# Two product-key expert layers: 64 down units during routing, both token tiles routed at once, one-hot rows token by token

## The chip, the cores and the metric

The kernel runs on one core of a Trainium2 chip, as one program of some 65,000 instructions. The metric is the device time of one execution in microseconds (us), the median of a few runs. The engines are named as the profile names them: PE is the Tensor engine (PEld its weight loads), DVE the Vector engine, ACT the Scalar engine, POOL GpSimd, SP the queue that issues the loads.

## The reference

256 tokens of width 1024 pass through two blocks. The first block has two layers, each a mixer and then a product-key expert layer, `peer_ffn`; the second block has no experts and is not touched here. The expert layer, cut to what matters:

```python
q = (xi @ w_query).reshape(B, PEER_CHUNK, PEER_HEADS, 2, PEER_HALF)     # 8 heads, 2 halves
s = jnp.einsum('bthpd,hpnd->bthpn', q, sub_keys)                         # 128 keys per half
s1, i1 = lax.top_k(s[..., 0, :], PEER_TOPK)                              # 16 best of each half
s2, i2 = lax.top_k(s[..., 1, :], PEER_TOPK)
cand = (s1[..., :, None] + s2[..., None, :]).reshape(..., 256)
top_s, top_c = lax.top_k(cand, PEER_TOPK)                                # 16 best pairs
idx = i1[top_c // 16] * 128 + i2[top_c % 16]
g = jax.nn.softmax(top_s, axis=-1)
act = jax.nn.gelu(einsum('btd,bthkd->bthk', xi, expert_down[idx]))
out = einsum('bthk,bthkd->btd', g * act, expert_up[idx])
```

There are 128 x 128 experts, and each of the 256 tokens chooses 8 x 16 of them.

## The kernel before

All experts are computed for all tokens, and the choice enters as a gate. The down and the up matrix are streamed in 128 units of 128 experts each, 512 KB a unit. One unit makes 24 matmuls of 256 columns: 8 chunks of the contraction, times three, since weights and data are split exactly into two parts, `whi`/`wlo` and `xnh`/`xnl` (`mm3`, L167 to L172). `Stream.unit` (L87) loads a unit (`raw`), ACT makes `whi` from it (L93), and DVE or POOL makes `wlo` = raw - whi (L97); the letters of `pattern` ("g" POOL, "v" DVE) say which of the two, unit by unit. `raw`, `whi` and `wlo` have three buffers each.

`peer` (L488) has four stretches.

1. *Query and scores.* 16 units of `wq` are multiplied with the tokens into `mm` banks. For every unit and each of two token tiles of 128, DVE looks for the 16 best of 128 scores: `top16`, five big instructions (L521 to L525) with three small loads of values.
2. *Ranks and keys.* For one token tile after the other: 54 candidate sums `cand`, `top16` over them for each of 8 heads, softmax gates `gt`, and the place in the candidate list turned into a pair of ranks `ra`, `rb` (L577 to L584), then into key numbers `key` by comparing with `iota`, multiplying and summing over `oh` (L593 to L599). PE transposes the result (`tp`) and DVE copies it to `it`: key numbers and gates with the tokens along the free axis.
3. *Down units kept.* The first `N_STORE` down units are multiplied during the first two stretches. Two units share a PSUM bank `dn`, ACT applies gelu and leaves them in `ca` (L607).
4. *One-hot.* For each of 64 groups of 4 tokens: `oa` is the one-hot row of the first key, `ob` that of the second key times the gate; PE multiplies the two (`gps`, L639, four products of 128 columns, each recorded as two matmuls), which gives the gate of every expert for each token. DVE multiplies the part of the kept units into `ca` (L641), ACT copies the rest to `gg` (L642). In every third group (`by_act`) ACT makes `ob` itself. `oa` and `ob` have three buffers.

L641 reads and writes a group's columns of all kept units at once, so no group can get past L641 before the last kept unit's gelu, and four banks for `gps` bound how far PE gets ahead. PE fills this stretch with `mod` matmuls of the second block (32 steps of four in layer 0) and with four "parked" down units (`N_PARK`). After it, down units that are left alternate with up units (`acc`), then up units alone, each 24 matmuls.

A scheduler sets the order of the instructions on each engine, by the order in which they are written, their dependencies and its own idea of how long they take; on the chip each engine works through its list in that order.

Of the kernel before, what the change touches and what calls it, by code (L numbers as in the profile page):

```python
# [22 lines left out]
N_STORE = 32  # L23
# [21 lines left out]
PAT_R = "g"  # L45
# [20 lines left out]
class Stream:  # L66
    """Weights streamed in tiles of 1024 columns, each split exactly in two float32r parts."""
# [33 lines left out]
class Net:  # L101
# [50 lines left out]
    def psum(self, **bufs):  # L152
        """the 8 banks by tag: "ac" accumulators, "fl" work for idle engines, the others in turn"""
# [25 lines left out]
    def proj_tok(self, ap, xn, out):  # L179
        """out[:, tt, :] = tokens x 256 columns, from two units of 4 contraction chunks."""  # L180
# [38 lines left out]
    def norm_stat(self, x, nr):  # L219
        """reciprocal root mean squares of the rows, on every partition"""  # L220
# [30 lines left out]
    def columns(self, r, pool):  # L251
        """rows of r (all alike) as one column per token tile"""
# [7 lines left out]
    def norm(self, x, gain, shift=None, pool=None, nr=None, r=None):  # L260
        """RMS-normalised rows, transposed, in two parts."""
# [42 lines left out]
# ------------------------------------------------------------------ first block, layer 0 mixer  # L304
def hgrn_gmlp(n: Net):
# [3 lines left out]
    with ExitStack() as st:  # L309
# [11 lines left out]
        # lower bound: first row of a softmax over three rows  # L321
# [38 lines left out]
        # scores S[s, h, t] by doubling blocks: every exponent is a sum of logs of f, never positive  # L360
# [51 lines left out]
        # token-major values of both halves  # L412
# [74 lines left out]
# ------------------------------------------------------------------ product-key experts  # L487
def peer(n: Net, layer, mod, mod_upto):  # L488
# [4 lines left out]
    with ExitStack() as st:  # L493
# [13 lines left out]
        with ExitStack() as sr:  # L507
# [6 lines left out]
            val = [r.tile([128, 16, 16], F32, name=f"val{t}") for t in range(2)]  # L514
            idx = [r.tile([128, 16, 16], U32, name=f"idx{t}") for t in range(2)]
            idf = [r.tile([128, 16, 16], F32, name=f"idf{t}") for t in range(2)]
            topv = [r.tile([128, 8, 16], F32, name=f"topv{t}") for t in range(2)]
            topc = [r.tile([128, 8, 16], U32, name=f"topc{t}") for t in range(2)]
# [8 lines left out]
            def score(j, qt):  # L527
# [4 lines left out]
                for tt in range(2):  # L532
                    tmp = r2.tile([128, 128], F32, tag="tmp", name="tmp")
                    top16(val[tt][:, j], idx[tt][:, j], sc[:, tt], tmp)
# [11 lines left out]
            score(*late)  # L546
            for tt in range(2):
                cand = r.tile([128, 8, NCAND], F32, tag="cand", name="cand")
                v4 = val[tt].rearrange("p (h s) k -> p h s k", s=2)
                for a0, a1, wb, o in CAND:  # L550
                    na = a1 - a0
                    nc.vector.tensor_tensor(
                        out=cand[:, :, o:o + na * wb].rearrange("p h (a b) -> p h a b", b=wb),
                        in0=v4[:, :, 0, a0:a1].unsqueeze(3).to_broadcast([128, 8, na, wb]),
                        in1=v4[:, :, 1, 0:wb].unsqueeze(2).to_broadcast([128, 8, na, wb]), op=OP.add)
                for h in range(8):
                    tmp = r2.tile([128, 128], F32, tag="tmp", name="tmp")
                    top16(topv[tt][:, h], topc[tt][:, h], cand[:, h], tmp[:, 0:NCAND])
                # gates
                gt = r.tile([128, 8, 16], F32, tag="gt", name="gt")  # L560
                gs = r.tile([128, 8], F32, tag="gs", name="gs")
                nc.vector.tensor_tensor(out=gt, in0=topv[tt], in1=topv[tt][:, :, 0:1].to_broadcast([128, 8, 16]),
                                        op=OP.subtract)
                nc.scalar.activation(out=gt, in_=gt, func=AF.Exp, scale=rc[:, tt:tt + 1])
                nc.vector.tensor_reduce(out=gs, in_=gt, axis=AX.X, op=OP.add)
                nc.vector.reciprocal(out=gs, in_=gs)
                nc.vector.tensor_tensor(out=gt, in0=gt, in1=gs.unsqueeze(2).to_broadcast([128, 8, 16]), op=OP.mult)
                # positions in the candidate list -> rank pairs -> key indices
                pos = r.tile([128, 8, 16], F32, tag="pos", name="pos")
                ra = r.tile([128, 8, 16], F32, tag="ra", name="ra")  # L570
# [1068 lines left out]
```

## Time and profile before

| | |
|---|---|
| median of 3 runs | 3510.65 us (3499.51 to 3512.86) |
| span of the profiled execution | 3511.2 us |
| PE busy | 3303.3 us, 94% of the span |
| DVE busy | 2213.6 us, 63% |
| ACT busy | 1665.6 us, 47% |
| POOL busy | 527.8 us, 15% |
| share of PE in the chain that ended last | 80%, of DVE 13% |

The span of the profiled execution stands for its whole time; nothing of note lies around it, and it is within 0.02% of the median. A busy PE is not one at its peak: matmuls are pipelined, and a record lasts about 0.28 us where the next one starts 0.117 us later. So matmuls are counted here, not added up. [...]

### The profile page before, as it was taken

How to read it: one execution, taken by the hardware profiler on the slowest of the kernel's cores; microseconds unless marked ns; L12 is line 12 of the kernel's file. 1: busy time of each engine (PE TensorE's matmuls, PEld its weight loads, DVE VectorE, ACT ScalarE, POOL GpSimd, SP SyncE). 2: the span in 40 equal slices, each digit the busy share in tenths (PEclk: the TensorE clock that was granted, in tenths of full speed). 3: DMA queues.
4: the chain of work that ended last, by engine and by line, in shares of the span. 5: the costliest groups of instructions: out<-in, count | busy, mean ns of one | idle time of the engine just before them, and what ended most of it. 6: DMA issues, size and time to landing. Idle time of an engine off the chain costs nothing.

```text
span 3511.2 us, 65248 instructions
## 1 busy us (share of the span) xinstructions
PE 3303.3 (94%) x26734; PEld 3151.3 (90%) x26734; DVE 2213.6 (63%) x4081; ACT 1665.6 (47%) x2613; POOL 527.8 (15%) x275
## 2 busy tenths in 40 slices
PE   7897989999999989699999999999999989999798
PEld 6787879999999779678999999899999779999698
DVE  6379785555555649887555555666675756666665
ACT  5444564444444344365444444544654544454443
POOL 2256430000000227541000000200000010100200
PEclk9998999999999999899999999999999989999899
DMA  6643545555555544365555555554444235455353
GB/s 223 231 155 117 169 160 185 199 186 181 185 182 187 199 156 150 104 201 195 200 184 182 185 182 185 198 186 159 144 163 156 91 108 187 161 184 167 130 183 108
DMA packets 165755, 597.75 MB, mean 170 GB/s; under 512 B 18512, under 2 KB 20176, under 8 KB 165072
## 3 DMA queue, kind: packets, MB, share of 16 engines
q1 hardware_dynamic: 165456, 593.59, 50.4%
q8 instruction: 209, 3.42, 0.4%
q14 instruction: 90, 0.74, 0.1%
HBM read 592.47 MB, written 1.05 MB: 169 GB/s over the span
## 4 chain that ended last, share of the span: by engine, by line
PE 80%; DVE 13%; ACT 2%; DMA 2%; issue 1%; POOL 1%; SPq 0%; ACTq 0%; DVEq 0%; POOLq 0%
PE acc L170 10%; PE acc L171 10%; PE acc L172 10%; PE ff L170 6%; PE ff L171 6%; PE ff L172 6%; PE dn L171 6%; PE dn L172 6%; PE dn L170 6%; PE mm L170 2%; PE mm L171 2%; PE mm L172 2%; DVE oa L621 2%; PE gps L639 2%; PE mod L940 1%
## 5 line engine op out<-in xcount | busy, mean ns | idle before, releaser
L93 ACT CAST whi<-raw 128x1024 fp32r<-128x1024 f32 x973 | 1015.6, 1046 | 1457.5 <-PE acc L171 541.7
L97 DVE TENSOR_TENSOR wlo<-raw,whi 128x1024 fp32r<-128x1024 f32 x812 | 999.7, 1232 | 839.7 <-ACT whi L93 839.4
L97 POOL TENSOR_TENSOR wlo<-raw,whi 128x1024 fp32r<-128x1024 f32 x161 | 392.7, 2446 | 2151.1 <-ACT whi L93 2131.5
L172 PE MATMUL dn<-xnh,wlo 128*128 128x256 f32 x2048 | 586.7, 287 | 11.4 <-POOL wlo L97 11.4
L170 PE MATMUL dn<-xnh,whi 128*128 128x256 f32 x2048 | 586.7, 286 | 4.0 <-ACT whi L93 4.0
L171 PE MATMUL dn<-xnl,whi 128*128 128x256 f32 x2048 | 585.6, 286 | 0.0
L171 PE MATMUL acc<-cl,whi 128*128 128x256 f32 x2048 | 570.4, 283 | 0.8 <-DVE cl L165 0.8
L172 PE MATMUL acc<-ch,wlo 128*128 128x256 f32 x2048 | 569.5, 283 | 0.0
L170 PE MATMUL acc<-ch,whi 128*128 128x256 f32 x2048 | 543.5, 283 | 0.0
L170 PE MATMUL ff<-xnh,whi 128*128 128x258 f32 x1760 | 505.2, 288 | 8.3 <-ACT whi L93 2.3
L171 PE MATMUL ff<-xnl,whi 128*128 128x258 f32 x1760 | 503.5, 286 | 7.7 <-DVE xnl L247 7.7
L172 PE MATMUL ff<-xnh,wlo 128*128 128x258 f32 x1760 | 500.6, 285 | 3.2 <-POOL wlo L97 1.9
L172 PEld LDWEIGHTS dn<-xnh,wlo 128*128 128x128 f32 x2048 | 398.9, 195 | 12.4 <-POOL wlo L97 12.4
L170 PEld LDWEIGHTS dn<-xnh,whi 128*128 128x128 f32 x2048 | 398.8, 195 | 4.8 <-ACT whi L93 4.8
L171 PEld LDWEIGHTS dn<-xnl,whi 128*128 128x128 f32 x2048 | 398.7, 195 | 0.0
L171 PEld LDWEIGHTS acc<-cl,whi 128*128 128x128 f32 x2048 | 393.4, 192 | 1.3 <-DVE cl L165 1.3
L172 PEld LDWEIGHTS acc<-ch,wlo 128*128 128x128 f32 x2048 | 393.1, 192 | 0.0
L170 PEld LDWEIGHTS acc<-ch,whi 128*128 128x128 f32 x2048 | 377.4, 192 | 0.0
L170 PEld LDWEIGHTS ff<-xnh,whi 128*128 128x128 f32 x1760 | 335.7, 191 | 12.9 <-ACT rstd L216 3.6
L171 PEld LDWEIGHTS ff<-xnl,whi 128*128 128x128 f32 x1760 | 338.1, 192 | 9.6 <-DVE xnl L247 9.0
L172 PEld LDWEIGHTS ff<-xnh,wlo 128*128 128x128 f32 x1760 | 336.4, 191 | 4.3 <-POOL wlo L97 2.1
L171 PE MATMUL acc<-hl,whi 128*128 128x256 f32 x880 | 245.8, 281 | 3.1 <-DVE hl L1017 3.1
(446 smaller groups left out, 5578.2 us busy)
## 6 DMA issues: line engine op xcount, KB each, us to landing
raw<-l_down SPq DMA_DIRECT2D x256, 512.0 KB, 3.3
raw<-l_up SPq DMA_DIRECT2D x256, 512.0 KB, 3.3
mraw<-w_mod SPq DMA_DIRECT2D x144, 512.0 KB, 4.3
raw<-f1i SPq DMA_DIRECT2D x132, 512.0 KB, 3.4
raw<-f2i SPq DMA_DIRECT2D x88, 512.0 KB, 4.1
raw<-f1o SPq DMA_DIRECT2D x66, 512.0 KB, 3.5
raw<-w_t SPq DMA_DIRECT2D x46, 512.0 KB, 4.0
raw<-f2o SPq DMA_DIRECT2D x44, 512.0 KB, 3.8
```

Source lines behind the costliest of these rows:

```text
L93: nc.scalar.copy(hi[:, 0:k], raw[:, 0:k])
L97: eng.tensor_tensor(out=low[:, 0:k], in0=raw[:, 0:k], in1=hi.bitcast(F32)[:, 0:k], op=OP.subtract)
L170: mm(out, w[0], x[0], start=first, stop=False, skip_group_check=True)
L171: mm(out, w[0], x[1], start=False, stop=False, skip_group_check=True)
L172: mm(out, w[1], x[0], start=False, stop=last, skip_group_check=True)
L621: nc.vector.tensor_tensor(out=dst, in0=n.iota.unsqueeze(1).to_broadcast([128, 4, 128]), in1=it[:, s, t0:t0 + 4].unsqueeze(2).to_broadcast( ...
L639: nc.tensor.matmul(g[:, t], a[:, t], b[:, t], start=t == 0, stop=True, skip_group_check=True)
L940: nc.tensor.matmul(ps[32 * j:32 * j + 32], n.cond[:, k], raw[:, j * T:(j + 1) * T], start=k == 0, stop=k == NDC - 1, tile_position=(0, 32 ...
```

## The change

`N_STORE` goes from 32 to 64: 64 down units are kept in `ca` and `gg` holds 64 in place of 96. `PAT_R` goes from "g" to "v": while an expert layer routes, DVE makes `wlo`, not POOL. The second stretch works on both token tiles at once: tiles of 16 rows (2 tiles x 8 heads) take the place of two rounds of 8, the ranks come from 18 instructions of 256 columns (before: 44 of 128 columns in each round), and `it` is complete only at the end. In the fourth stretch each token gets an instruction of its own for `oa` and for `ob`, with the key (and the gate) as one number per partition; the product with the gate by POOL is gone. Docstrings and comments are removed as well, which is left out here.

```diff
-N_STORE = 32
+N_STORE = 64
...
-PAT_R = "g"
+PAT_R = "v"
...
-            for tt in range(2):
-                cand = r.tile([128, 8, NCAND], F32, tag="cand", name="cand")
...
-                for a in range(2, 16):
-                    step = r2.tile([128, 8, 16], F32, tag="step", name="step")
-                    nc.vector.tensor_scalar(out=step, in0=pos, scalar1=float(starts[a][0]), scalar2=None, op0=OP.is_ge)
-                    nc.vector.tensor_tensor(out=ra, in0=ra, in1=step, op=OP.add)
-                    nc.vector.scalar_tensor_tensor(out=rb, in0=step, scalar=-float(starts[a - 1][1]), in1=rb,
-                                                   op0=OP.mult, op1=OP.add)
...
+            cand = r.tile([128, 16, NCAND], F32, name="cand")
...
+            nc.vector.tensor_scalar(out=ra, in0=pos, scalar1=-float(starts[8]), scalar2=0.0, op0=OP.add, op1=OP.max)
+            nc.vector.scalar_tensor_tensor(out=rb, in0=ra, scalar=-1.0, in1=pos, op0=OP.mult, op1=OP.add)
+            for a0, a1, wb, o in CAND[:-1]:
+                run = r.tile([128, 16, 16], F32, tag="run", name="run", bufs=2)
+                for i, s0 in enumerate(starts[a0 + 1:a1 + 1]):
+                    if i == 0:
+                        nc.vector.tensor_scalar(out=run, in0=pos, scalar1=float(s0), scalar2=None, op0=OP.is_ge)
+                    else:
+                        nc.vector.scalar_tensor_tensor(out=run, in0=pos, scalar=float(s0), in1=run,
+                                                       op0=OP.is_ge, op1=OP.add)
+                nc.vector.tensor_tensor(out=ra, in0=ra, in1=run, op=OP.add)
+                nc.vector.scalar_tensor_tensor(out=rb, in0=run, scalar=-float(wb), in1=rb, op0=OP.mult, op1=OP.add)
...
-                def equal(s, dst):
-                    nc.vector.tensor_tensor(out=dst, in0=n.iota.unsqueeze(1).to_broadcast([128, 4, 128]),
-                                            in1=it[:, s, t0:t0 + 4].unsqueeze(2).to_broadcast([128, 4, 128]),
-                                            op=OP.is_equal)
...
-                    equal(1, b)
-                    nc.gpsimd.tensor_tensor(out=b, in0=b, op=OP.mult,
-                                            in1=it[:, 2, t0:t0 + 4].unsqueeze(2).to_broadcast([128, 4, 128]))
+                for t in range(4):
+                    at = lambda s: it[:, s, t0 + t:t0 + t + 1]
+                    nc.vector.tensor_scalar(out=a[:, t], in0=n.iota, scalar1=at(0), scalar2=None, op0=OP.is_equal)
...
+                        nc.vector.tensor_scalar(out=b[:, t], in0=n.iota, scalar1=at(1), scalar2=at(2),
+                                                op0=OP.is_equal, op1=OP.mult)
```

On DVE in the second stretch of layer 0, where the ranks are made, before (line numbers of the kernel before; `topc`, `topv`: the best candidates):

```order
L583 TENSOR_TENSOR ra<-ra,step 128x128
L584 SCALAR_TENSOR_TENSOR rb<-step,rb 128x128
L582 TENSOR_SCALAR step<-pos 128x128
L525 MAX_INDEX topc_1854<-topv_1852,tmp 128x8
L523 MATCH_REPLACE tmp<-topv_1852,cand 128x54
L582 TENSOR_SCALAR step<-pos 128x128
```

and after (line numbers of the changed kernel, where L585 to L590 make `run`, `ra` and `rb`):

```order
L97 TENSOR_TENSOR wlo<-raw,whi 128x1024
L571 TENSOR_TENSOR gt<-gt,gs 128x256
L589 TENSOR_TENSOR ra<-ra,run 128x256
L590 SCALAR_TENSOR_TENSOR rb<-run,rb 128x256
L589 TENSOR_TENSOR ra<-ra,run 128x256
L97 TENSOR_TENSOR wlo<-raw,whi 128x1024
L590 SCALAR_TENSOR_TENSOR rb<-run,rb 128x256
L585 TENSOR_SCALAR run<-pos 128x256 x2
L587 SCALAR_TENSOR_TENSOR run<-pos,run 128x256 x2
L97 TENSOR_TENSOR wlo<-raw,whi 128x1024
```

A weight split (L97) now stands on DVE after every few instructions of the routing; before there was none between the first score and the copy to `it`, POOL had them. In the changed kernel 16 splits of `wq` and 32 of down units stand on DVE ahead of the copies to `it`, and 36 more (32 kept and 4 parked) behind them.

On PE at the end of the routing of layer 0, after:

```order
L171 MATMUL dn<-xnl,whi 128x256
L639 MATMUL gps<-ob,oa 128x128 x8
L172 MATMUL dn<-xnh,wlo 128x256
L170 MATMUL dn<-xnh,whi 128x256
L171 MATMUL dn<-xnl,whi 128x256
L172 MATMUL dn<-xnh,wlo 128x256
```

Behind these eight products of the one-hot stretch come 740 `dn` matmuls in a row, nearly 31 units, before the next `gps`. Before, the first `gps` of layer 0 stood behind 19 of 36 units, and the second token tile's routing ran beside the other 17.

On DVE in the one-hot stretch of layer 0, before:

```order
L621 TENSOR_TENSOR oa<-iota,it 128x512
L641 TENSOR_TENSOR ca<-ca,gps 128x32x4
L621 TENSOR_TENSOR oa<-iota,it 128x512
L621 TENSOR_TENSOR ob<-iota,it 128x512
L641 TENSOR_TENSOR ca<-ca,gps 128x32x4
```

and after (L631 makes `oa`, L636 makes `ob`):

```order
L631 TENSOR_SCALAR oa<-iota,it 128x128 x4
L641 TENSOR_TENSOR ca<-ca,gps 128x64x4
L631 TENSOR_SCALAR oa<-iota,it 128x128
L636 TENSOR_SCALAR ob<-iota,it 128x128
L631 TENSOR_SCALAR oa<-iota,it 128x128
L636 TENSOR_SCALAR ob<-iota,it 128x128
L631 TENSOR_SCALAR oa<-iota,it 128x128
L636 TENSOR_SCALAR ob<-iota,it 128x128
L631 TENSOR_SCALAR oa<-iota,it 128x128
L636 TENSOR_SCALAR ob<-iota,it 128x128
L641 TENSOR_TENSOR ca<-ca,gps 128x64x4
```

Four instructions stand where one stood, and L641 covers 64 units (256 columns) in place of 32. The lag of L641 behind the groups that it closes is the same two to three groups. Layer 1 has the same pattern, with 40 `mod` steps.

## Rows read from the trace of the kernel before

**Rows 1.** The page: its first line, and the busy time of PE.

```profile
span 3511.2 us, 65248 instructions
PE 3303.3 (94%) x26734; PEld 3151.3 (90%) x26734; DVE 2213.6 (63%) x4081; ACT 1665.6 (47%) x2613; POOL 527.8 (15%) x275
```

**Rows 2.** Stretches: length, busy PE, PEld, DVE, ACT, POOL, granted clock, DMA share, GB/s.

```profile
240.00:260.00 20.00, 20.00 (x171) 20.00 (x171) 15.42 (x93) 7.65 (x11) 14.51 (x7) 1.00 0.47 157
300.00:320.00 20.00, 8.26 (x50) 8.26 (x51) 19.52 (x60) 2.59 (x3) 3.99 (x2) 0.58 0.06 20
340.00:360.00 20.00, 11.19 (x70) 10.69 (x69) 19.55 (x36) 4.73 (x6) 10.18 (x5) 0.69 0.35 119
440.00:460.00 20.00, 17.58 (x163) 11.95 (x162) 19.62 (x38) 13.72 (x41) 9.89 (x8) 1.00 0.73 235
```

**Rows 3.** Timeline of PE: start, length, first of each stretch, layers 0 and 1.

```profile
192.33 0.77 PE L170 MATMUL mm<-xnh,whi 128*128 128x256 f32 x1
...
251.71 0.28 PE L170 MATMUL dn<-xnh,whi 128*128 128x256 f32 x1
...
508.32 0.40 PE L170 MATMUL acc<-ch,whi 128*128 128x256 f32 x2
...
1302.13 0.47 PE L170 MATMUL mm<-xnh,whi 128*128 128x256 f32 x1
...
1619.00 0.40 PE L170 MATMUL acc<-ch,whi 128*128 128x256 f32 x2
```

**Rows 4.** Tile `ca`: min/median/max ns, first and last start.

```profile
L641 DVE TENSOR_TENSOR ca<-ca,gps x128: 269/275/290, 391.7 to 1615.6; 128x128 f32<-128x128 f32 x128
```

**Rows 5.** Weight splits by line (min/median/max ns), then DVE's groups from 200 to 392.

```profile
L97 DVE TENSOR_TENSOR wlo<-raw,whi x812: 680/1225/3262, 16.2 to 3481.0; 128x1024 fp32r<-128x1024 f32 x162, 128x512 fp32r<-128x512 f32 x1
...
L97 POOL TENSOR_TENSOR wlo<-raw,whi x161: 1841/2402/3462, 14.6 to 3317.9; 128x1024 fp32r<-128x1024 f32 x159, 128x768 fp32r<-128x768 f32 x2
...
L583 DVE TENSOR_TENSOR ra<-ra,step 128x128 f32<-128x128 f32 x28 | 18.3, 652 | 0.0
...
L596 DVE TENSOR_TENSOR oh<-oh,idf 128x1024 f32<-128x1024 f32 x4 | 9.0, 2248 | 0.1
...
L525 DVE FIND_INDEX8 topc<-topv,tmp 128x8 uint32<-128x54 f32 x16 | 3.2, 204 | 0.0
```

**Rows 6.** Timeline of DVE: between these, seven searches and four loads; then one-hot.

```profile
199.79 0.29 DVE L522 FIND_INDEX8 idx<-val,mm 128x8 uint32<-128x128 f32 x1
...
201.45 1.73 DVE L217 RECIPROCAL rstd<-rstd 128x256 f32<-128x256 f32 x1
...
442.08 0.68 DVE L621 TENSOR_TENSOR oa<-iota,it 128x512 f32<-128x512 f32 x1
442.68 0.68 DVE L621 TENSOR_TENSOR ob<-iota,it 128x512 f32<-128x512 f32 x1
443.28 0.27 DVE L641 TENSOR_TENSOR ca<-ca,gps 128x128 f32<-128x128 f32 x1
```

**Rows 7.** DVE's groups from 392 to 510: busy us, mean ns.

```profile
L621 DVE TENSOR_TENSOR oa<-iota,it 128x512 f32<-128x512 f32 x57 | 56.1, 984 | 0.0
```

**Rows 8.** TENSOR_SCALAR by form, whole span: constant; number per partition; two such numbers.

```profile
L577 DVE TENSOR_SCALAR ra<-pos 128x128 f32<-128x128 f32 x4 | 0.8, 210 | 0.0
...
L705 DVE TENSOR_SCALAR pr<-pr,sm 128x256 f32<-128x256 f32 x8 | 2.8, 348 | 0.0
L705 DVE TENSOR_SCALAR pr<-pr,sm 128x128 f32<-128x128 f32 x8 | 2.3, 286 | 0.2
...
L348 DVE TENSOR_SCALAR lf<-lf,lbo,lbv x4: 412/642/1228, 22.1 to 36.8; 128x256 f32<-128x256 f32 x4
```

**Rows 9.** Timeline of PE in the one-hot stretch, and a window at half clock.

```profile
442.70 0.64 PE L940 MATMUL mod<-mraw,cond 128*32 128x256 f32 x8
443.27 0.94 PE L639 MATMUL gps<-ob,oa 128*128 128x128 f32 x6
...
485.00:490.00 5.00, 3.78 (x16) 3.49 (x16) 5.00 (x9) 1.85 (x5) 1.77 (x2) 0.50 0.59 196
```

More of the change, by code (lines that the diff above doesn't have):

```diff
@@ L513, in peer @@
             nc.sync.dma_start(out=keys, in_=d[pre + "keys"])
[L514 to L518, printed above, removed]
+            val = r.tile([128, 2, 16, 16], F32, name="val")
+            idx = r.tile([128, 2, 16, 16], U32, name="idx")
+            idf = r.tile([128, 2, 16, 16], F32, name="idf")
+            topv = r.tile([128, 16, 16], F32, name="topv")
+            topc = r.tile([128, 16, 16], U32, name="topc")
             def top16(vals, pos, src, tmp):
@@ new lines, in peer @@
+            v4 = val.rearrange("p t (h s) k -> p (t h) s k", s=2)
+            i4 = idf.rearrange("p t (h s) k -> p (t h) s k", s=2)
+            nc.vector.tensor_copy(out=idf, in_=idx)
+            cand = r.tile([128, 16, NCAND], F32, name="cand")
+            for a0, a1, wb, o in CAND:
+                na = a1 - a0
+                nc.vector.tensor_tensor(
+                    out=cand[:, :, o:o + na * wb].rearrange("p h (a b) -> p h a b", b=wb),
+                    in0=v4[:, :, 0, a0:a1].unsqueeze(3).to_broadcast([128, 16, na, wb]),
+                    in1=v4[:, :, 1, 0:wb].unsqueeze(2).to_broadcast([128, 16, na, wb]), op=OP.add)
@@ new lines, in peer @@
+            for h in range(16):
+                tmp = r2.tile([128, 128], F32, tag="tmp", name="tmp")
+                top16(topv[:, h], topc[:, h], cand[:, h], tmp[:, 0:NCAND])
+            gt = r.tile([128, 16, 16], F32, name="gt")
+            gs = r.tile([128, 16], F32, name="gs")
+            nc.vector.tensor_tensor(out=gt, in0=topv, in1=topv[:, :, 0:1].to_broadcast([128, 16, 16]),
+                                    op=OP.subtract)
+            for tt in range(2):
+                hs = slice(8 * tt, 8 * tt + 8)
+                nc.scalar.activation(out=gt[:, hs], in_=gt[:, hs], func=AF.Exp, scale=rc[:, tt:tt + 1])
@@ new lines, in peer @@
+            nc.vector.tensor_reduce(out=gs, in_=gt, axis=AX.X, op=OP.add)
+            nc.vector.reciprocal(out=gs, in_=gs)
+            nc.vector.tensor_tensor(out=gt, in0=gt, in1=gs.unsqueeze(2).to_broadcast([128, 16, 16]), op=OP.mult)
+            pos = r.tile([128, 16, 16], F32, name="pos")
+            nc.vector.tensor_copy(out=pos, in_=topc)
+            starts = [o + i * wb for a0, a1, wb, o in CAND for i in range(a1 - a0)]
+            ra = r.tile([128, 16, 16], F32, name="ra")
+            rb = r.tile([128, 16, 16], F32, name="rb")
@@ new lines, in peer @@
+            key = r.tile([128, 2, 16, 16], F32, name="key")
+            oh = r.tile([128, 16, 128], F32, name="oh")
+            for s, rank in ((0, ra), (1, rb)):
+                for k0, k1 in ((0, 4), (4, 8), (8, 16)):
+                    nk = k1 - k0
+                    o = oh[:, :, 0:nk * k1].rearrange("p h (k j) -> p h k j", j=k1)
+                    nc.vector.tensor_tensor(out=o, in0=rank[:, :, k0:k1].unsqueeze(3).to_broadcast([128, 16, nk, k1]),
+                                            in1=n.iota[:, 0:k1].unsqueeze(1).unsqueeze(1).to_broadcast([128, 16, nk, k1]),
+                                            op=OP.is_equal)
+                    nc.vector.tensor_tensor(out=o, in0=o,
+                                            in1=i4[:, :, s, 0:k1].unsqueeze(2).to_broadcast([128, 16, nk, k1]),
+                                            op=OP.mult)
+                    nc.vector.tensor_reduce(out=key[:, s, :, k0:k1], in_=o, axis=AX.X, op=OP.add)
@@ L600, in peer @@
+            for tt in range(2):
+                hs = slice(8 * tt, 8 * tt + 8)
                 tp = n.bank("tp")
-                for i, src in enumerate((key[:, 0], key[:, 1], gt)):
+                for i, src in enumerate((key[:, 0, hs], key[:, 1, hs], gt[:, hs])):
                     nc.tensor.transpose(tp[:, i * 128:(i + 1) * 128], src.rearrange("p h k -> p (h k)"), n.ident)
@@ L618, in peer @@
                 g = n.bank("gps").rearrange("p (t e) -> p t e", t=4)
[L620 to L623 removed]
                 by_act = t0 // 4 % N_ACT == 1
[L626 to L637 removed]
+                for t in range(4):
+                    at = lambda s: it[:, s, t0 + t:t0 + t + 1]
+                    nc.vector.tensor_scalar(out=a[:, t], in0=n.iota, scalar1=at(0), scalar2=None, op0=OP.is_equal)
+                    if by_act:
+                        nc.scalar.activation(out=b[:, t], in_=n.iota, func=AF.Abs, scale=-1.0, bias=at(1))
+                        nc.scalar.activation(out=b[:, t], in_=b[:, t], func=AF.Relu, scale=-2.0, bias=at(2))
+                    else:
+                        nc.vector.tensor_scalar(out=b[:, t], in0=n.iota, scalar1=at(1), scalar2=at(2),
+                                                op0=OP.is_equal, op1=OP.mult)
                 for t in range(4):
```

53 lines of the change are left out of this document (1 added, 52 removed).

## Prediction, on record before the changed kernel ran

> **What bounds the kernel now.** The page says that PE is busy for 3303.3 of 3511.2 us [rows 1]; no gain comes from less matmul work, since the change removes none. So I looked at stretches, first by busy time and instruction counts. Where nothing disturbs it, PE starts 171 matmuls in 20 us [rows 2], one every 0.117 us, so a unit of 24 takes 2.81 us. Between 300 and 320, and between 340 and 360, it makes 50 and 70, at a mean granted clock of 0.58 and 0.69 (part of the time at 1.2 GHz, behind idle stretches), while DVE is busy throughout [rows 2]. There the routing on DVE is awaited, and the 32 down units that could have filled PE are used up or stand behind the transposes of the keys. Then comes the one-hot stretch, where DVE is again busy for 19.62 of 20 us [rows 2].
>
> The timeline gives the ends. In layer 0 the query starts at 192.33, the first down unit at 251.71, and the first up unit, behind the one-hot stretch, at 508.32: 316.0 us. In layer 1 it is 1302.13 to 1619.00, 316.9 us [rows 3]. The first L641, which needs all kept units, starts at 391.7 [rows 4], so about 117 us of the 316 are one-hot work and 199 are query, routing and down units. Outside these stretches the change moves nothing of size.
>
> **The cost of DVE's instructions.** Instructions that follow each other start earlier than the rows' durations say: 0.68 us of L621 lead to a start 0.60 us later, twice [rows 6]. A turn on DVE is a row's duration less about 0.08 us. By that a split takes 1.14 us of DVE (median 1.225) [rows 5], and L641 0.20 us (0.275) [rows 4].
>
> **Splits from POOL to DVE.** POOL needs 2.40 us a split, DVE 1.14 [rows 5]. While POOL works, DVE's own instructions stretch: L583 over 128 columns takes 0.652 us on average, L596 over 1024 columns 2.248 [rows 5], where a 512-column instruction takes 0.68 [rows 6]. POOL's 80 splits and 43 gate products of a layer go, and so does the stretching. DVE gets 80 splits in exchange: 16 + 64 times 1.14, 91 us.
>
> **Can DVE carry both?** In the query stretch, until the last `wq` split, it has 16 splits (18 us), some 21 of the 32 searches over 128 scores, and about 8 us of normalisation. Seven big instructions and four loads took 1.66 us, so a search of five and three takes 1.2 [rows 6]: 25 us. Together 51 us, and PE took 59 before (192.33 to 251.71) [rows 3]; I take 62 after, for both layers, since DVE comes close. From there to the copies to `it`, DVE has 11 searches (13 us); 16 searches over 54 candidates, five times 0.12 and three times 0.06, 0.8 us each (duration 0.204) [rows 5], 13 us; 28 us of sums, ranks and key selection, the latter by six passes over 2048 columns at 2.2 us each; and 32 splits (36 us): 90 us. PE needs 32 times 2.81, 90 us, for the same units. So both are full, and neither waits long. A split that is late makes PE wait, and in DVE's list splits are spaced by at most about 6 us against PE's 2.8, with three buffers between. A split that waits for a buffer holds back the routing behind it, but the keys are needed only by PE's transposes, and behind those 36 units are left, for which DVE has time to spare. I take 7 us of stalls a layer; the bounds are 0 and 25 (a quarter more DVE work in 98 us of routing, all of it on the path).
>
> **64 units kept.** The kept units end after 62 + 64 x 2.81 (180) + 7 = 249 us, in place of 199. The 32 additional ones leave the later stretch, where units run one after the other: 32 x 2.81, 90 us less there. This part alone gains 199 + 90 - 249 = 40 us a layer. It is PE's idle time and its time at 1.2 GHz that is filled.
>
> **One-hot rows.** The trace of before has no comparison with a number per partition over 128 columns, but the same kind of instruction: L705 with one such number takes 286 ns at 128 columns, 348 at 256 [rows 8]; a constant in its place (L577) 210 [rows 8]. L348 has two numbers at 256 columns, 412 ns at the least [rows 8], 64 more than one. So `oa` is a turn of 0.20, `ob` 0.27 (286 + 64 - 83). L641 doubles to 256 columns: 0.33. Of 64 groups 43 have their `ob` from DVE:
>
> 256 x 0.20 + 172 x 0.27 + 64 x 0.33 = 51 + 46 + 21 = 118 us.
>
> Some five groups are made ahead, while PE still has down units (-7 us); two splits and the `mod` sums come in (+4 us); to the first up unit pass another 3. That makes 118, against 117 before. The old form was cheaper (0.60 for 512 columns [rows 6]), but it lasted 0.984 on average [rows 7], since POOL's product ran beside it. So this edit gains nothing by itself; POOL's contention goes and 4 times as many instructions come. Lower bound: a turn as with a constant, 0.13, for both: 428 x 0.13 + 21 = 77 us. PE would then be the bound. A `gps` group of 8 takes 0.9 to 1.0 us and a `mod` step up to 0.57 (442.70 to 443.27) [rows 9], 64 + 18 + 11 for the parked units = 93. Upper bound: 0.26 and 0.33, as the rows at 256 columns: 67 + 57 + 21 = 145, 27 us more.
>
> [...]
>
> **Sum.** A layer: 62 + 180 + 7 + 118 = 367 us, against 316 + 90 = 406: 39 us less. Two layers: 78. 3511 - 78 = 3433 us, against a median (3510.65) that equals the span.
>
> **Rivals.**
> *Dearer one-hot rows.* A number per partition might cost more in a comparison, or two of them might. At the upper bound the gain falls by 27 a layer to 12: 3487 us. For it: the form is not in the trace. Against: L705 and L577 differ by 76 ns only [rows 8], so one number costs little.
> *Cheaper ones, PE bound.* One-hot in 93 us gains 25 more a layer: 3383 us. [...]
> *Splits too late.* DVE is full in the routing; 25 us of stalls in place of 7 leave 21 a layer: 3469 us. For it: 90 us of work in 90 us. Against: behind the keys there is slack.
> *The one-hot stretch at half clock (slower than before).* All additional down units now stand ahead of it, and PE has gaps in it. Before, between 485 and 490, the clock was 0.50 and 16 matmuls took 3.78 us of PE, 0.236 each [rows 9]. At that a layer's 512 + 256 + 96 records, the `mod` ones at four in parallel, take 64 x 1.9 + 32 x 1.1 + 96 x 0.236 = 179 us, and PE bounds: 61 us more a layer, 3511 - 2 x (39 - 61) = 3555 us. It decides from 118 + 39 = 157 us of one-hot work on. Against: at 440 to 460, with 163 matmuls in 20 us, the clock was 1.00 [rows 2]; after, there are about 130, more than the 70 at 0.69.
>
> **Chances.** The forecast 0.62 (own range 3410 to 3455), dearer 0.12, cheaper 0.09, late splits 0.12, half clock 0.05. What can be told from no change is about 0.5%, 17 us; 3487 is just beyond it, so half of that case counts as no difference. Faster 0.62 + 0.09 + 0.12 + 0.06 = 0.89, same 0.06, slower 0.05. The range goes from the cheaper case to the dearer one, 3385 to 3487, and leaves out half clock and the edges of these two.
>
> **What would show it.** Right: 170 matmuls per 20 us at a clock of 1.00 from the first down unit until all 64 are done, some 245 us behind the query's start; first up unit about 367 us behind it; no POOL in either layer's routing; `oa` at 0.28 us, `ob` at 0.35, L641 at 0.41. Wrong: PE waiting for L97 by DVE within the routing, durations above 0.35 for `oa`, a granted clock below 0.9 in the one-hot stretch, or a stretch of `mod` matmuls that waits for its loads there.

## The result and the profile after

The changed kernel takes 3459.06 us (median of four runs, 3456.91 to 3467.64) where the kernel before, in the same session, takes 3511.76: a ratio of 0.987, 95% interval [0.984, 0.990]. By the medians it is faster by 53 us, by the ratio, for which one disturbed run of the kernel before (6347.74 us) is left out, by 46; 78 were forecast. The profiled execution is the slowest of the four, 8.6 us above the median; differences of a few us in one stretch of it should not be read as more than that.

On the page POOL's work has gone from 527.8 to 179.0 us [rows 1]:

```profile
span 3465.9 us, 65621 instructions
PE 3313.4 (96%) x26734; PEld 3150.2 (91%) x26734; DVE 2193.9 (63%) x4589; ACT 1649.2 (48%) x2609; POOL 179.0 (5%) x93
```

PE's timeline, the same places as in [rows 3] (first query matmul, first down unit, first up unit, of layers 0 and 1):

```profile
192.35 0.78 PE L170 MATMUL mm<-xnh,whi 128*128 128x256 f32 x1
...
248.89 0.28 PE L170 MATMUL dn<-xnh,whi 128*128 128x256 f32 x1
...
574.46 0.54 PE L170 MATMUL acc<-ch,whi 128*128 128x256 f32 x3
...
1275.86 0.47 PE L170 MATMUL mm<-xnh,whi 128*128 128x256 f32 x1
...
1336.95 0.28 PE L170 MATMUL dn<-xnh,whi 128*128 128x256 f32 x1
...
1669.89 0.28 PE L170 MATMUL acc<-ch,whi 128*128 128x256 f32 x1
```

From query to first up unit pass 382.1 and 394.0 us (forecast: 367). Then the instructions of the one-hot stretch, by tile (minimum, median, maximum ns, first and last start), which answer to [rows 4] and to the forecast durations of 0.28, 0.35 and 0.41:

```profile
L641 DVE TENSOR_TENSOR ca<-ca,gps x128: 400/412/422, 445.6 to 1657.4; 128x256 f32<-128x256 f32 x128
...
L631 DVE TENSOR_SCALAR oa<-iota,it x512: 268/279/289, 343.5 to 1649.6; 128x128 f32<-128x128 f32 x171
...
L636 DVE TENSOR_SCALAR ob<-iota,it x344: 328/340/350, 343.7 to 1649.8; 128x128 f32<-128x128 f32 x172
```

The windows of [rows 2], with two more (length, busy PE, PEld, DVE, ACT, POOL, granted clock, DMA share, GB/s):

```profile
240.00:260.00 20.00, 20.00 (x172) 20.00 (x171) 20.00 (x96) 7.62 (x12) 0.00 (x0) 1.00 0.48 158
300.00:320.00 20.00, 20.00 (x169) 20.00 (x168) 18.75 (x21) 9.33 (x11) 0.00 (x0) 1.00 0.54 178
340.00:360.00 20.00, 20.00 (x171) 20.00 (x170) 15.51 (x41) 12.47 (x25) 0.00 (x0) 1.00 0.57 182
385.00:405.00 20.00, 20.00 (x169) 20.00 (x168) 8.45 (x7) 9.16 (x11) 0.00 (x0) 1.00 0.53 183
...
560.00:580.00 20.00, 17.03 (x111) 15.93 (x110) 14.31 (x32) 6.31 (x12) 0.00 (x0) 0.83 0.40 132
```

Two things are to be seen. In the four windows up to 405 PE makes 169 to 172 matmuls at a clock of 1.00, where it made 50 and 70 in those from 300 and from 340. And DVE falls to 8.45 of 20 us well before the kept units end: from about 350 on the routing is finished (the last copy to `it` starts at 341.9), and PE works off kept units that nothing waits behind but L641. So does the gain come from the 64 units, or from the shorter routing? And why is the one-hot stretch 129 and 136 us long, with every duration as forecast?

The first L641 to the first up unit, layer 0 and layer 1 (windows as above):

```profile
445.55:574.46 128.91, 113.30 (x867) 85.36 (x866) 115.25 (x470) 72.24 (x225) 0.00 (x0) 0.95 0.46 152
1533.53:1669.89 136.36, 120.09 (x933) 87.61 (x931) 117.83 (x478) 73.04 (x225) 0.00 (x0) 0.94 0.53 173
```

and what PE and DVE wait for there, 445 to 575 (us in total, times, longest):

```profile
PE mod L940 <- DMA mraw<-w_mod: 7.4, 8, 1.8
...
DVE ca L641 <- PE gps L639: 12.6, 9, 3.0
```

DVE waits 12.6 us for PE's `gps`, and PE, at the head of its queue, waits 7.4 us for the loads of `mod` steps. The first theory made of it: the `mod` loads hold PE up, and with it DVE.

### The profile page after: what moved, and what is told of

Its sections match the earlier page's. It is cut to its first block, busy times and chain, and to the rows that moved or that the text cites. A ratio compares the mean times of both kernels' runs of the same rounds, so it can differ in the third digit from the quotient of the medians.

```text
span 3465.9 us, 65621 instructions
## 1 busy us (share of the span) xinstructions
PE 3313.4 (96%) x26734; PEld 3150.2 (91%) x26734; DVE 2193.9 (63%) x4589; ACT 1649.2 (48%) x2609; POOL 179.0 (5%) x93
## 4 chain that ended last, share of the span: by engine, by line
PE 83%; DVE 11%; DMA 2%; ACT 2%; issue 1%; POOL 0%; SPq 0%; ACTq 0%; DVEq 0%; POOLq 0%
PE acc L170 11%; PE acc L171 10%; PE acc L172 10%; PE dn L172 7%; PE dn L170 7%; PE dn L171 7%; PE ff L170 6%; PE ff L171 6%; PE ff L172 6%; DVE wlo L97 2%; PE mm L170 2%; PE mm L171 2%; PE mm L172 2%; PE mod L940 2%; DMA mraw<-w_mod 2%; PE gps L639 2%
## 5 line engine op out<-in xcount | busy, mean ns | idle before, releaser
L97 DVE TENSOR_TENSOR wlo<-raw,whi 128x1024 fp32r<-128x1024 f32 x908 | 1111.6, 1225 | 841.8 <-ACT whi L93 841.3
L171 PE MATMUL acc<-cl,whi 128*128 128x256 f32 x2048 | 561.6, 283 | 1.0 <-DVE cl L165 1.0
L172 PE MATMUL acc<-ch,wlo 128*128 128x256 f32 x2048 | 559.5, 283 | 0.0
L170 PE MATMUL acc<-ch,whi 128*128 128x256 f32 x2048 | 512.2, 283 | 0.2 <-DVE gg L667 0.2
L170 PEld LDWEIGHTS acc<-ch,whi 128*128 128x128 f32 x2048 | 363.7, 192 | 0.4 <-DVE gg L667 0.4
L97 POOL TENSOR_TENSOR wlo<-raw,whi 128x1024 fp32r<-128x1024 f32 (+1 forms) x65 | 157.7, 2433 | 2614.0 <-ACT whi L93 1968.6
```

What stands on the lines that cost most here:

```text
L97: eng.tensor_tensor(out=low[:, 0:k], in0=raw[:, 0:k], in1=hi.bitcast(F32)[:, 0:k], op=OP.subtract)
L170: mm(out, w[0], x[0], start=first, stop=False, skip_group_check=True)
L171: mm(out, w[0], x[1], start=False, stop=False, skip_group_check=True)
L172: mm(out, w[1], x[0], start=False, stop=last, skip_group_check=True)
```

## The experiments

All times in this table come from the profiled execution of each kernel, read from the starts of PE's timeline and of L641; "kept" is first down unit to first L641, "one-hot" from there to the first up unit, "later" from there to the last up matmul, each layer 0 / layer 1. The last column is the ratio of the timed runs to the kernel before, with its 95% interval.

| kernel | kept | one-hot | later | median us | ratio |
|---|---|---|---|---|---|
| before | 140.0 / 140.2 | 116.6 / 114.6 | 628.7 / 628.7 | 3510 to 3512 | 1 |
| changed | 196.7 / 196.6 | 128.9 / 136.4 | 537.3 / 536.6 | 3459.1 | 0.987 [0.984, 0.990] |
| e1: before, 64 kept | 230.0 / 229.9 | 127.8 / 131.7 | 536.6 / 537.4 | 3531.6 | 1.006 [1.005, 1.007] |
| e2: changed, 32 kept | 101.2 / 102.0 | 120.8 / 125.4 | 628.7 / 628.7 | 3446.4 | 0.982 [0.980, 0.983] |
| e3: changed, POOL splits | 212.0 / 212.0 | 127.1 / 136.0 | 537.3 / 536.6 | 3497.5 | 0.996 [0.995, 0.998] |
| e4: changed, old one-hot | 193.9 / 195.9 | 132.1 / 127.3 | 537.2 / 537.2 | 3460.6 | 0.986 [0.984, 0.988] |
| e5: before, DVE splits | 102.6 / 102.7 | 136.8 / 136.1 | 629.3 / 629.3 | 3477.2 | 0.992 [0.990, 0.993] |
| e6: before, merged routing | 120.3 / 120.3 | 120.0 / 120.3 | 629.3 / 628.7 | 3484.2 | 0.993 [0.992, 0.994] |
| e7: changed, mod steps away | 196.7 / 196.6 | 115.5 / 115.5 | 537.0 / 538.2 | 3581.2 | 1.020 [1.018, 1.022] |
| e8: changed, fresh mod banks | 196.7 / 195.7 | 130.6 / 138.2 | 537.0 / 537.7 | 3469.5 | 0.988 [0.986, 0.990] |
| e9: changed, no mod loads | 196.7 / 195.7 | 130.5 / 132.6 | 537.0 / 537.8 | 3467.2 | 0.987 [0.986, 0.989] |
| e10: e2 with `oa` at once | 100.7 / 100.7 | 110.3 / 123.0 | 629.4 / 628.7 | 3431.6 | 0.976 [0.974, 0.978] |
| e11: e2 with old one-hot | 101.6 / 104.9 | 121.7 / 118.4 | 628.7 / 628.7 | 3438.8 | 0.979 [0.978, 0.980] |
| e12: changed, `oa` at once | 195.8 / 196.2 | 112.6 / 118.8 | 537.3 / 536.6 | 3436.2 | 0.978 [0.977, 0.980] |

**e1, the number of kept units alone**, on the kernel before:

```diff
-N_STORE = 32
+N_STORE = 64
```

> The kernel before with 64 kept down units as its only change. Account of the prediction (the kept units fill PE's idle time in the routing, which lasts 199 us from the query's start to the first L641 anyway): 62 + 64 x 2.81 = 242 us to the first L641, some 245 to 250 with stalls, and 90 us less later: 40 to 45 us a layer, 3420 to 3435 us. Rival (the old routing in two passes, with POOL's splits beside it, is slowed by twice as many splits): first L641 265 us or more behind the query's start, gain at most 24 us a layer, 3463 us or more. Either way the one-hot stretch stays near 117 us.

The prediction's account falls: the kernel gets slower, by 21 us. The first L641 moves back by 90 us, from 140 to 230, the later stretch gets 91 to 92 shorter, and the one-hot stretch 11 to 17 longer. The rival's bounds hold (first L641 288 us behind the query's start), but not its reason, as the windows show. Windows of e1, two in the routing and two behind it (columns as above):

```profile
285.00:305.00 20.00, 7.88 (x66) 7.67 (x64) 19.83 (x69) 3.70 (x5) 9.46 (x4) 0.75 0.36 127
...
325.00:345.00 20.00, 14.01 (x100) 13.36 (x98) 19.93 (x37) 13.50 (x25) 15.25 (x7) 0.86 0.24 80
...
365.00:385.00 20.00, 20.00 (x169) 20.00 (x168) 0.00 (x0) 9.14 (x11) 16.01 (x8) 1.00 0.51 174
...
445.00:465.00 20.00, 20.00 (x169) 20.00 (x169) 0.00 (x0) 8.67 (x11) 16.70 (x7) 1.00 0.53 184
```

The holes in the routing are still there, 66 and 100 matmuls in 20 us; the 32 additional units run when DVE has nothing to do at all. The waits of e1's PE from 280 to 365 say why:

```profile
PE tp L602 <- DVE key L599: 20.1, 2, 15.4
```

The kernel before has the same row, 20.1 us, between 250 and 392. PE stands at the transposes of the keys, and what could fill the time stands behind them in its list: 25 down units stand ahead of the last of them, with 64 kept units as with 32.

**e2, the other way round**: the changed kernel with 32 kept units.

```diff
-N_STORE = 64
+N_STORE = 32
```

> The changed kernel with 32 kept units, as before the change. If the new routing's DVE work is what I summed (62 us of query, then about 90 of routing and splits), it ends at 152 to 160 us, where 32 units of PE (62 + 90) end too: then 32 units do as well as 64, and the run takes what the changed kernel takes, 3455 to 3475 us: the two edits are then each other's substitutes. If the gain needs the 64 units, PE idles in the routing as before, the first L641 comes at 185 us or later, and the run takes 3500 us or more.

It is 13 us faster than the changed kernel, better than either account allowed, and the two intervals do not meet. In the routing PE is full with 32 units:

```profile
285.00:305.00 20.00, 20.00 (x169) 20.00 (x168) 19.20 (x61) 11.82 (x15) 0.00 (x0) 1.00 0.54 186
...
325.00:345.00 20.00, 20.00 (x169) 20.00 (x169) 18.83 (x28) 11.08 (x18) 0.00 (x0) 1.00 0.55 185
```

and its L641 takes 0.278 us, not 0.412. So the 64 units give nothing: 95 us more in front, 91 to 92 less later, and the wider L641 on top.

**e3, who makes the splits**: the changed kernel with POOL's.

```diff
-PAT_R = "v"
+PAT_R = "g"
```

> The changed kernel with the experts' splits on POOL again. If DVE had time for them under PE's units (my account), nothing is gained by freeing 91 us of DVE a layer: first L641 still 247 to 258 us behind the query's start and 3450 to 3470 us; a split of 2.40 us on POOL stays under PE's 2.81 a unit. If POOL's contention with DVE was what made the old routing slow, DVE's rows stretch again and the first L641 comes 15 us or more later: 3490 us or more. If DVE's splits do hold PE back, the run is faster: 3445 us or less.

The times are those of the second account: 15 us more a layer to the first L641, and a ratio of 0.996 in place of 0.987. DVE's groups of e3 from 252 to 345 (busy us, mean ns):

```profile
L631 DVE TENSOR_SCALAR oa<-iota,it 128x128 f32<-128x128 f32 x14 | 10.6, 782 | 0.0
...
L636 DVE TENSOR_SCALAR ob<-iota,it 128x128 f32<-128x128 f32 x9 | 7.3, 809 | 0.0
L604 DVE TENSOR_REDUCE key<-oh 128x64 f32<-128x256 f32 (+2 forms) x6 | 6.8, 1131 | 0.2
```

A comparison for `oa` takes 782 ns on average where the changed kernel's takes 279; the reduction beside it is not touched (1131, against 1126 ns in the changed kernel). And the first rank instruction, over the whole span of e3, takes anything from its own time (284 to 287 ns in the changed kernel) to that of a POOL split (34 of them take 82.54 us in e3's window below, 2.43 each; minimum, median, maximum):

```profile
L585 DVE TENSOR_SCALAR run<-pos x8: 285/1310/2497, 280.7 to 1389.8; 128x256 f32<-128x256 f32 x8
```

So the stretching is real. But even with it DVE is done sooner than in the changed kernel. The last keys, on DVE's timeline of e3 and of the changed kernel:

```profile
324.92 2.29 DVE L604 TENSOR_REDUCE key<-oh 128x128 f32<-128x2048 f32 x1
```

```profile
336.03 2.28 DVE L604 TENSOR_REDUCE key<-oh 128x128 f32<-128x2048 f32 x1
```

That is 75.2 us behind e3's first down unit, and 89.4 behind the changed kernel's. DVE's busy time from the query's start to these ends, in e3, then in the changed kernel, whole and for its splits (L97) alone:

```profile
192.49:327.21 134.72, 115.96 (x916) 114.10 (x914) 119.77 (x452) 54.23 (x79) 82.54 (x34) 0.93 0.36 126
```

```profile
192.35:338.33 145.98, 142.34 (x1167) 141.04 (x1165) 135.75 (x493) 67.93 (x95) 0.00 (x0) 0.99 0.47 155
...
192.35:338.33 145.98, 52.16 (x44) 0.00 (x0) 0.99 0.47 155
```

The stretching costs DVE an estimated 36 us (119.8, less 135.8 - 52.2), the splits cost it 52. Yet it is e3's PE that waits for the keys (the only row of its waits from 250 to 465):

```profile
PE tp L609 <- DVE key L604: 14.4, 2, 14.0
```

The order differs. In e3 14.7 down units stand ahead of the first key transposes in PE's list and 18.8 ahead of the last, in the changed kernel 24.1 and 30.1 (matmuls of `dn` before them, by 24): moving the splits has also moved the transposes. With the splits on DVE the keys come later, but PE has enough to do until then.

**e4, the old one-hot rows** in the changed kernel:

```diff
-                    nc.vector.tensor_scalar(out=a[:, t], in0=n.iota, scalar1=at(0), scalar2=None, op0=OP.is_equal)
+                equal(0, a)
...
-                        nc.vector.tensor_scalar(out=b[:, t], in0=n.iota, scalar1=at(1), scalar2=at(2),
-                                                op0=OP.is_equal, op1=OP.mult)
+                    equal(1, b)
+                    nc.gpsimd.tensor_tensor(out=b, in0=b, op=OP.mult,
+                                            in1=it[:, 2, t0:t0 + 4].unsqueeze(2).to_broadcast([128, 4, 128]))
```

> The changed kernel with the old one-hot rows (one comparison over 512 columns, the gate product on POOL). The changed kernel's stretch from the first L641 to the first up unit is 129 and 136 us, 11 and 18 more than my 118. Theory 1 (PE's mod steps stand in bursts and wait for their loads, the gps matmuls behind them): the form hardly matters, the stretch stays at 125 to 137 us, and the run at 3450 to 3465 us. Theory 2 (DVE's many small instructions set the stretch): it falls to about the 114 to 117 us of the kernel before, and the run to 3425 to 3440 us.

No difference, and the stretch is where theory 1 puts it: the new form is worth nothing by itself. But two forms that cost DVE and its partners the same would give this too.

**e5 and e6, the two halves of the shorter routing**, each on the kernel before. e5 has DVE's splits only:

```diff
-PAT_R = "g"
+PAT_R = "v"
```

> The kernel before with the experts' splits on DVE as its only change. Theory A (POOL's splits run beside DVE and stretch its instructions two to three times, as the rows of e3 show: the comparison for oa 782 ns there, 279 in the changed kernel): the routing loses its stretching, first L641 110 to 125 us behind the first down unit where the kernel before has 140, and 3465 to 3490 us. Rival B (the merged routing code is what shortens it; splits on DVE only add 36 us of DVE work): 140 us or more, and 3510 us or more.

e6 has the new second stretch only; against the changed kernel:

```diff
-N_STORE = 64
+N_STORE = 32
...
-PAT_R = "v"
+PAT_R = "g"
...
+                    nc.gpsimd.tensor_tensor(out=b, in0=b, op=OP.mult,
+                                            in1=it[:, 2, t0:t0 + 4].unsqueeze(2).to_broadcast([128, 4, 128]))
```

(with the other lines of e4.)

> The kernel before with the routing of both token tiles at once as its only change: 32 kept units, splits on POOL, the old one-hot rows. Theory A (contention is the larger part): first L641 118 to 130 us behind the first down unit (e3's 212 less 90 for 32 units is 122), 3470 to 3495 us. Rival B (the merged code alone does it): 101 to 108 us, as in e2, and 3435 to 3450 us. Nothing gained (140 us, 3510 us) if DVE's stretched passes are as long in either form.

Both runs take the time that theory A gave them: 32 us are gained by the splits, 25 by the merged routing. But in e5 the first L641 comes at 102.6, sooner than its 110 to 125, and DVE's routing does not end sooner, as theory A wants: the last keys are found 7 us later than before. On DVE's timeline of the kernel before, and of e5:

```profile
364.16 1.22 DVE L599 TENSOR_REDUCE key<-oh 128x64 f32<-128x1024 f32 x1
```

```profile
373.46 1.22 DVE L599 TENSOR_REDUCE key<-oh 128x64 f32<-128x1024 f32 x1
```

What goes with PE's wait for the keys is the order of its list (layer 0; us, and down units):

| kernel | last keys behind first down unit | down units ahead of first / last key transposes | PE's wait for keys |
|---|---|---|---|
| before | 113.7 | 13.6 / 25.1 | 20.1 |
| e5 | 120.6 | 23.5 / 36.0 | 0.2 |
| e6 | 75.2 | 14.7 / 18.8 | 14.9 |
| e3 | 75.2 | 14.7 / 18.8 | 14.4 |
| changed | 89.4 | 24.1 / 30.1 | none |

The merged routing brings the keys 38 us sooner (e6). The splits on DVE bring them later, and in both forms of the routing 9 to 11 more units come to stand ahead of the transposes. The scheduler set these orders; that it counts DVE's time for the splits, but not the stretching, would explain them and is not shown. No run changes the order alone.

In e5 the kept units end as early as in e2, but the one-hot stretch is 20 us longer than before: DVE still has the second token tile's keys to find when L641 could begin, so its lateness shows one stretch later. Of the twelve products for the keys (two tiles of six) six lie behind the first L641, in DVE's groups of e5 from 356 to 493:

```profile
L596 DVE TENSOR_TENSOR oh<-oh,idf 128x128 f32<-128x128 f32 (+2 forms) x6 | 3.9, 646 | 0.2
```

In e6 PE still waits at the key transposes, with 18.8 units ahead of the last and DVE's passes stretched as in e3 (L585 at 1347 ns on average, 1349 there; waits of e6's PE from 250 to 370):

```profile
PE tp L609 <- DVE key L604: 14.9, 2, 14.0
```

Together (e11) they gain 74 us, more than 32 + 25: one alone leaves the other's limit standing.

**e7, the one-hot stretch without mod steps**; they are made later, in the stage that makes the rest, and the whole gets longer for it:

```diff
-N_MOD = 32
+N_MOD = 0
...
-                    peer(n, int(s[4]), mods[1], N_MOD if s[4] == "0" else 72)
+                    peer(n, int(s[4]), mods[1], 0)
```

> The changed kernel without the mod steps in the one-hot stretch; they are done later, in the stage that does the rest of them, so the whole time says little, and the stretch from the first L641 to the first up unit is what is read (129 and 136 us in the changed kernel). Theory 1 (PE's mod steps, which wait for their loads ahead of the gps matmuls, make the overrun over my 118): 105 to 118 us in both layers, and no wait for w_mod. Theory 2 (DVE's small instructions cost more than I summed): 125 us or more in both.

Both layers have 115.5 us; layer 0's window, and what DVE waits for in it:

```profile
447.17:562.65 115.48, 99.20 (x602) 79.89 (x601) 112.73 (x457) 73.96 (x225) 0.00 (x0) 0.99 0.07 24
```

```profile
DVE ca L641 <- PE gps L639: 2.4, 1, 2.4
```

Without `mod` DVE is all but full (112.73 of 115.48 us) and sets the stretch, at the sum of its turns. So the 13 and 21 us above come with the mod steps. Their order or their loads?

**e8, no bursts**:

```diff
         if self.bank is None:
             self.bank = n.bank("mod", self.tag)
...
+            if self.tag == "ac":
+                self.bank = None
```

> The changed kernel with a fresh PSUM bank for each group of eight mod steps, where all groups share one. By the order PE's program then has single mod steps among the gps groups, where it has bursts of three behind each group of eight. Theory 1 (the bursts wait for their loads): the waits for w_mod fall below 4 us a layer, the stretch from the first L641 to the first up unit to 115 to 124 us, the run to 3430 to 3450 us. Theory 2 (DVE sets the stretch): 129 to 136 us as before, 3452 to 3466 us.

The bursts are gone, the waits for the loads are not (8.8 and 13.0 us on PE), and neither stretch is shorter. The bursts were not it.

**e9, mod steps without loads**:

```diff
-        raw = tile_p.tile([128, 1024], F32, tag="raw", name="mraw")
-        nc.sync.dma_start(out=raw, in_=n.d["w_mod"][self.l, i, k])
+        if self.tag == "ac":
+            raw = n.x.rearrange("p c t -> p (c t)")[:, 0:1024]
+        else:
+            raw = tile_p.tile([128, 1024], F32, tag="raw", name="mraw")
+            nc.sync.dma_start(out=raw, in_=n.d["w_mod"][self.l, i, k])
```

> The changed kernel with its mod steps in place, but without their loads: the same matmuls, sums and copies read the resident x in place of w_mod (so the modulation vectors that the second layer's last stages use are not the reference's). Read is the stretch from the first L641 to the first up unit: 129 and 136 us in the changed kernel, 115.5 in both layers without any mod step (e7). If the loads make the overrun: 115 to 121 us in both layers, and a run of 3430 to 3448 us. If it is the steps' own work on PE and DVE, their transposes and the bank that they share: 125 us or more in both, and 3452 us or more.

The windows of both layers, and DVE's wait in layer 0's:

```profile
444.13:574.67 130.54, 120.58 (x866) 89.95 (x865) 116.25 (x471) 72.82 (x225) 0.00 (x0) 0.96 0.08 25
1534.41:1666.99 132.58, 124.10 (x937) 90.31 (x936) 117.63 (x479) 72.66 (x225) 0.00 (x0) 0.97 0.08 25
```

```profile
DVE ca L641 <- PE gps L639: 12.8, 13, 2.4
```

With no load to wait for, layer 0's stretch is as long as ever and layer 1's 4 us shorter, and DVE waits 12.8 us where it waited 12.6. Theory 1 falls: the wait for the loads was, but for at most those 4 us, time that PE would have lost anyway, and the row that named it misled me. What is left is the steps' own work, most of it on PE, ahead of the `gps` that DVE wants, with DVE already full. The granted clock is a small part of it: at 0.97, as in layer 1 here, it takes at most 3% of 132.6 us, an estimated 4 us, from a stretch that is 17 longer than e7's.

**e10 to e12, less work for DVE.** e12 is the changed kernel with one comparison over 512 columns for `oa`, e10 the same with 32 kept units:

```diff
+                nc.vector.tensor_tensor(out=a, in0=n.iota.unsqueeze(1).to_broadcast([128, 4, 128]),
+                                         in1=it[:, 0, t0:t0 + 4].unsqueeze(2).to_broadcast([128, 4, 128]),
+                                         op=OP.is_equal)
...
-                    nc.vector.tensor_scalar(out=a[:, t], in0=n.iota, scalar1=at(0), scalar2=None, op0=OP.is_equal)
```

> 32 kept units, both routing edits, and oa by one comparison over 512 columns a group again (0.60 us a turn in the kernel before) where four over 128 columns take 4 x 0.20; ob stays with one instruction a token, and POOL stays idle. DVE saves 64 x 0.20 = 13 us a layer. If DVE sets the one-hot stretch (as in e7): 108 to 114 us in place of e2's 121 and 125, and 3420 to 3430 us. If the waits for the mod loads set it: 118 us or more, and 3437 to 3449 us, as e2.

> The changed kernel, 64 kept units, with oa by one comparison over 512 columns a group in place of four over 128; nothing else. DVE is relieved of 13 us a layer, PE of nothing. If PE and DVE are both nearly full in the one-hot stretch and each waits for the other (DVE busy 121 and PE 120 to 125 us of 129 and 136): 4 to 11 us less a layer, 118 to 125 and 128 to 133 us, and a run of 3437 to 3452 us, 10 to 20 us above e10. If PE with its mod steps alone sets the stretch: 127 us or more in both, 3455 us or more. If DVE alone sets it: 13 us less in both, 116 and 123 us, and 3433 us.

e11 is e4 with 32 kept units.

> 32 kept units, both routing edits, and the one-hot rows as in the kernel before (512 columns by one comparison, the product on POOL): the part of the change that e2 adds to it is the new one-hot form alone. My sum had the two forms equal at about 117 us. Equal: within 8 us of e2's 3446 us. If the new form is dearer by its waits: 3430 to 3438 us, the stretch at 114 to 118 us; if POOL's product costs more: 3455 us or more.

e12's window of layer 0, DVE's wait in it, and the turns of `oa` (0.60 us) and of four `ob` on DVE's timeline:

```profile
444.27:556.92 112.65, 99.36 (x873) 80.52 (x873) 105.50 (x299) 72.75 (x225) 0.00 (x0) 0.98 0.49 174
```

```profile
DVE ca L643 <- PE gps L641: 5.9, 8, 2.0
```

```profile
481.45 0.68 DVE L629 TENSOR_TENSOR oa<-iota,it 128x512 f32<-128x512 f32 x1
482.05 1.11 DVE L638 TENSOR_SCALAR ob<-iota,it 128x128 f32<-128x128 f32 x4
```

Twelve us less of DVE (64 times 0.18, four turns of 0.196 against one of 0.602) make the profiled stretch 16 and 18 us shorter, the run 23 us faster: that is "DVE sets it", and a little more, since DVE also waits 7 us less for PE. I had expected less from a stretch in which PE is nearly full as well. e10 gains 15 us over e2 and is the fastest kernel of the study, 2.4% below the kernel before; its layer 1, with 40 mod steps, still has 123.0 us, outside the 108 to 114 that I expected. In e11 the old rows are 8 us faster than e2's new ones, just beyond the intervals (0.9802 and 0.9804 are the nearest ends): no gain from the new form there either.

## Why the prediction was right, and where it was not

**The gain and its size.** Faster, as forecast; the sum was 26 us too hopeful, and 3459 lies in the range (3385 to 3487), 4 us above the forecast's own (3410 to 3455). The failed step is in the part on 64 kept units: "This part alone gains 199 + 90 - 249 = 40 us a layer", by filling PE's idle time and its time at what the prediction calls 1.2 GHz (a granted clock of 0.50; in the trace of before a matmul of 256 columns starts every 0.213 us at it, from 312.23 to 316.49, which is 1.2 columns a ns). It alone loses: 21 us in e1, and 13 us between e2 and the changed kernel. What my sum compared was 199 us of the old routing with 249 of the new; the 249 is nearly as forecast (253.2 and 257.7 us from query to first L641, no POOL, clock 1.00 from the first down unit on), but the 40 us come from the two routing edits, with which 32 kept units reach the first L641 about 101 us behind the first down unit (e2) where they took 140. Then PE is full up to there (busy for 100.9 of 101.2 us in layer 0 of e2), and every further unit only changes its place. That the total came out near is partly luck: the sum priced all edits of that stretch at once and gave the gain to the one that has none. My own front part had what was needed to see it: nearly 31 units stand behind the keys' transposes in PE's list, where nothing has to be hidden.

**Splits on DVE.** Right: they fit under PE's units (0.3 us of waits for L97 between 250 and 445), and the last keys come 89.4 and 86.0 us behind the first down unit, where I had 90 us of DVE work. To leave them out is dearer than I said, some 35 us (e3 against the changed kernel). The prediction has the stretching go with POOL, and it goes (`oa` at 279 ns, 782 in e3); but DVE does not find the keys sooner for it. What is saved is PE's wait for them, with 30 units and not 19 ahead of the last transposes. How POOL's splits would do with that order stays open. Not every instruction stretches: in e3 L585 takes 285 to 2497 ns beside splits of 2.43 us on average, while the reductions (1131 ns, 1126 in the changed kernel) and the searches over 54 scores (L525: 208, 206) keep their times. What decides which instruction is held up is not shown.

**One-hot rows.** The prices were right: turns (start to start in an unbroken run) of 0.196, 0.256 and 0.331 us where I had 0.20, 0.27 and 0.33. 256 x 0.196 + 172 x 0.256 + 64 x 0.331 = 115 us, and e7 has 115.5 (the corrections of my sum, -7, +4 and +3, cancel). That the form gains nothing by itself is right too (e4). The term that was mis-sized is the 118 as a whole: 129 and 136 in the profiled run. I added 4 us for two splits and the `mod` sums on DVE and compared DVE's 118 with PE's 93, as if the larger alone counted. The mod steps cost 13 and 21 us in a stretch in which DVE has no slack (e7). Neither their bursts (e8) nor, but for at most 4 us in layer 1, their loads (e9) are the reason. The granted clock is not the main one: 0.95 and 0.94 in the changed kernel, 0.99 and 1.00 in e7, but 0.97 in e9's layer 1, which is still 17 us longer. That leaves the steps' own work, above all on PE ahead of `gps`; it costs less where DVE has slack (112.6 and 118.8 us in e12, with the same steps). How the rest divides in the changed kernel stays open.

Of the two forms of `oa` the old one is the cheaper where POOL is idle: four comparisons over 128 columns take 0.78 us of DVE, one over 512 columns 0.60, and e12 gains 23 us by going back to it. The prediction had the 0.60 and set against it the 0.984 that the old form lasted beside POOL's product [rows 7]; in e12, without that product, it lasts 0.681 on average.

**The rivals.** Dearer or cheaper rows and late splits are refuted by the rows above. Half clock came in part: 0.95 and 0.94 over the stretches and 0.83 from 560 to 580, which is below the 0.9 that the prediction named as a sign of being wrong, but far from the 0.50 that the rival wanted. A stretch of `mod` matmuls that waits for its loads, which the prediction named as a sign of being wrong, was there, and e9 shows that it was not the cause, but for a few us.

**The sum, once more.** By the profiled execution, against the forecast: kept units end 4 and 9 us late, the one-hot stretch is 11 and 18 us longer, the later stretch gains 91 and 92 in place of 90, and the rest of the program is about 5 us shorter: 78 - 13 - 29 + 4 + 5 = 45, which is 3511.2 less 3465.9.

## What to carry to other kernels

Work kept as filler helps only if the order puts it ahead of the instruction that waits: count how much of it stands there, and ask what the stage would take with less of it. Giving a task to another engine can move that order too: before the gain is put down to faster instructions, look whether the awaited one ends any sooner. When two edits meet in one stretch, price each with the other in place and with it absent; here the two routing edits were worth 32 and 25 us alone and 74 together, and the 64 units less than nothing. A wait that the trace names at the head of a queue is a suspect only: take it away before believing it, above all where another engine in the stretch has no slack.

## What was not expected of the hardware

In the changed kernel a comparison over 128 columns with one number per partition turns over in 0.196 us, one with two such numbers, a comparison and a product, in 0.256: the second costs 0.060 us, as much as 128 further columns in L705 (62 ns, [rows 8]). POOL's splits in e3 stretch DVE's comparisons for `oa` to 2.8 times their length on average (782 against 279 ns), but not its reductions or searches (1131 against 1126 ns, and 208 against 206 for L525 over 54 scores). DVE was still sooner done with the keys beside POOL's splits than with the splits on its own list (75.2 against 89.4 us behind the first down unit).
